# Where a hybrid decoder block copies its index queries, builds its last rotation tables and places its attention, and in which PSUM banks its feed-forward sums start

## The chip, the cores and the metric

One core of a Trainium2 chip runs the whole kernel. The metric is device time in microseconds (us) of one execution. TensorE (PE) multiplies matrices into PSUM, which the kernel divides into eight banks of 512 columns; VectorE (DVE) and ScalarE (ACT) do elementwise work; SyncE (SP) issues the DMA transfers. Each engine works through its own queue in order, so an instruction that waits holds up everything behind it on its engine.

## The reference

One decoder layer over 256 tokens of width 2048, in float32:

```
proj = h @ w_in            # u (1024), q (8x128), k (2x128), v (2x128), index q (16x64), index k (64), index w (16)
y_ssm:  S5 state-space scan over time for 64 groups of 16 channels, 64 complex states each;
        gelu, then y * sigmoid(y @ w_glu + b_glu)
y_attn: score = sum_h wi_h * relu(qi_h . ki), causal; each token keeps its 64 best keys;
        softmax over the kept keys with a distance penalty (ALiBi), 8 heads over 2 key/value heads
h = layer_norm(alpha*h + concat(y_ssm, y_attn) @ w_out)
f = (gelu(conv3(h @ w_up)) * (h @ w_gate)) @ w_down      # width 5632, causal conv of width 3
out = layer_norm(alpha*h + f)
```

## The kernel before, in words

**Number format and weights.** Every large product is made from two float32r parts of each operand, a high part (a rounded copy) and a low part (the rest), in three matmuls: high by high, low by high, high by low (`mm3`, lines 186 to 188; `wide_half`, line 206, in the feed-forward part). Weights come in 512 KB halves by DMA into one of three `raw` buffers; ACT makes the high part `wh` (line 133), DVE the low part `wl` by a subtraction (line 136). Four halves are kept ahead of their use.

**Order of the work.** Python issues the instructions in program order; a planner then lists them for each engine from its own estimates, by priority and by what is ready. `tc.high_priority()` lifts what is inside it, `tc.issue_after(x)` puts instructions behind `x` on x's engine, and `tc.manual_schedule` keeps program order on the engines that it names. Side work (the state-space job, the indexer, the GLU's inputs) is written as Python generators: `pump()` moves them on by one `yield` after each `mm3`.

**Projections.** `ws_tile` (line 310) makes one 128 x 256 column tile of the projection from 16 x 3 matmuls in one of two PSUM banks called `acc`, then issues a copy out of it (`evac`) with high priority. In order: the last two state inputs u6 and u7, eight tiles of index queries (`index_four`, line 659; here `evac` is `split`, line 180: ACT copies the high part out of the bank, DVE subtracts to get the low part, both read the bank), the index keys and weights `kw`, the keys k0, the doubled index keys `kp` (line 715, copied out to `kps` at lines 721 to 724), k1, v, and the two times four query tiles q0 and q1. `proj_tile` notes its copy in the list `evacs`.

**State-space job** (`ssm`, line 638). It goes through four blocks of channels, bi = 0 to 3. For each, `ssm_in` (line 554) moves inputs by 16 small DMAs into `ustk`, builds the rotation tables (`angles`, line 382: eight small ACT copies at line 379, two DVE operations at lines 385 and 386, three ACT operations), the decay table `dec` (eight more ACT copies at line 379), then 32 small matmuls into `bu` (line 585), then twelve DVE operations (lines 595 to 609) with two scans (602, 603), which leave the states' real and imaginary halves (line 606 ends the one, line 609 the other). `ssm_out` (line 613) multiplies them into outputs (lines 623 and 629). The tables of blocks 1 to 3 share one buffer `cs`, and all decay tables share `dec`, so a new table waits for the block before: `cs` for line 608, `dec` for line 603.

**Indexer** (line 674). For each half of the tokens it adds up 16 heads of scores (lines 694 to 702) and finds the 64 largest by eight rounds on DVE (lines 705 to 708).

**Attention and output projection.** Four pieces a00, a10, a01, a11 (head group, half of the tokens) have four steps each: `scores` (PE line 766, DVE lines 770 to 773), `weights` (ACT exponentials, DVE normalisation at line 784), `turn` (PE transposes at line 791 into a `misc` bank, ACT copies out), `values` (PE line 800). There are two `misc` banks for all of them. The output projection is a run of units, each of 6 matmuls of 512 columns (line 992); the dictionary `beside` (line 976) says ahead of which unit an attention step stands. PE's order is by hand here.

**Feed-forward part.** The first four gate blocks are computed as rows beside the end of the output projection (`gacc`, in two of the four `o` banks of pool `pso`), copied to SBUF (line 1067) and transposed into tiles `gt` of the pool `pe0`. The up and gate sums use the four banks of pool `pd`. The pools `ps` (acc and misc) and `pso` are closed before; `pe0` is opened first and so gets the four banks at the left end, `pd` the four behind, where the `o` banks were.

Of the kernel before, what the change touches and what calls it, by code (L numbers as in the profile page):

```python
# [82 lines left out]
def block_kernel(ctx: ExitStack, tc: tile.TileContext, x_t, x_n, prm_d, cst_d, ssm_d, w_u_d, w_in_d, w_kw_d, w_v_d,  # L83
# [4 lines left out]
    def pool(name, bufs=1, **kw):  # L88
        return tc.tile_pool(name=name, bufs=bufs, **kw)
# [215 lines left out]
    for _ in range(WARM):  # L305
        T.matmul(wp, lhsT=warm[:, :P], rhs=warm, start=True, stop=True)

    last_mm = []

    def ws_tile(evac, m=P):  # L310

# [6 lines left out]
            pump()  # L318
        with tc.high_priority():
            return evac(acc)  # L320

    evacs = []

    def proj_tile(name, t=None):
        if t is None:
# [10 lines left out]

    def u_tile(ct, acc):
        t = proj.tile([P, 2, P], F32, name=f"u{ct}")
        A.activation(t.rearrange("p two k -> p k two"), acc.rearrange("p (k two) -> p k two", two=2), AF.Copy)
        ut.append(t)  # L340

    bu = psb.tile([P, 2, 2, 512], F32, name="bu")
# [31 lines left out]
    def by_pair(out, a, bi, row):  # L374

        for s_ in range(2):
            for ch in range(4):
                i = bi * 8 + ch * 2 + s_
                ins = A.activation(out[:, s_, ch * 128:(ch + 1) * 128], row, AF.Copy, scale=a[:, i:i + 1])
        return ins.ins  # L380
# [173 lines left out]
    def ssm_in(bi):  # L554

        ustk = st.tile([P, 2, 2, P], F32, name="ustk")
        for c in range(2):
            for h in range(2):
                for sd in range(2):
                    q = 2 * h + sd  # L560
                    for e in range(2):
                        r = 64 * sd + 32 * e
                        nc.sync.dma_start(out=ustk[r:r + 32, c, h, :], in_=ut[2 * bi + c][32 * q:32 * q + 32, 1 - e, :])  # L563

        def t4(name):
            return st.tile([P, 2, 512], F32, name=name)

        if bi == 0:
            c, s = tab
        else:  # L570
            cs = st.tile([P, 2, 2, 512], F32, name="cs")
            c, s = cs[:, 0], cs[:, 1]
            angles(bi, c, s)
        dec = t4("dec")
        with tc.issue_after(last_angle):
            by_pair(dec, r2, bi, cc("after0"))
        yield
        bu = psb.tile([P, 2, 2, 512], F32, name="bu")
        for c_ in range(2):
            for h in range(2):  # L580
                k = (c_ * 2 + h) * 128
                for sd in range(2):
                    r = slice(64 * sd, 64 * sd + 64)
                    for ri in range(2):
                        T.matmul(bu[:, sd, ri, k:k + 128], lhsT=bt[r, 2 * bi + c_, h, ri, :], rhs=ustk[r, c_, h, :],
                                 start=True, stop=True)
                        yield
        bre, bim = bu[:, :, 0, :], bu[:, :, 1, :]
        t3, t5 = t4("t3"), t4("t5")
        if bi % 2 == 0:  # L590
            t1, t2 = t4("t1a"), t4("t2a")
        else:
            t12 = st.tile([P, 2, 2, 512], F32, name="t12b")
            t1, t2 = t12[:, 0], t12[:, 1]
        V.tensor_tensor(t1, bre, c, op=ALU.mult)
        V.tensor_tensor(t2, bim, s, op=ALU.mult)
        V.tensor_tensor(t3, bim, c, op=ALU.mult)
        V.tensor_tensor(t5, bre, s, op=ALU.mult)
        V.tensor_tensor(t1, t1, t2, op=ALU.add)
        V.tensor_tensor(t3, t3, t5, op=ALU.subtract)  # L600
        fl = lambda t: t.rearrange("p q k -> p (q k)")
        V.tensor_tensor_scan(fl(t2), fl(dec), fl(t1), initial=0.0, op0=ALU.mult, op1=ALU.add)
        V.tensor_tensor_scan(fl(t5), fl(dec), fl(t3), initial=0.0, op0=ALU.mult, op1=ALU.add)
        V.tensor_tensor(t1, t2, c, op=ALU.mult)
        V.tensor_tensor(t3, t5, s, op=ALU.mult)
        V.tensor_tensor(t1, t1, t3, op=ALU.subtract)
        V.tensor_tensor(t2, t2, s, op=ALU.mult)
        V.tensor_tensor(t5, t5, c, op=ALU.mult)
        V.tensor_tensor(t2, t2, t5, op=ALU.add)
        hs[bi] = (t1, t2)  # L610
        yield
# [47 lines left out]
    def index_four(name, low_tag):  # L659
        parts = [proj.tile([P, 4, S], F32R, name=name + n, tag=tag) for n, tag in (("h", name), ("l", low_tag))]  # L660
        tiles = [(parts[0][:, i], parts[1][:, i]) for i in range(4)]
        for h, l in tiles:
            ws_tile(lambda acc: split(h, l, acc[:, :S]))
        return tiles

    qit = index_four("qi0", "qi0l") + index_four("qi1", "q1")
# [53 lines left out]
    with tc.high_priority():  # L720
        A.activation(kps[:, :S], kp[:, :S], AF.Copy)
        for b in range(2):
            bs = slice(S + b * 128, S + b * 128 + 80)
            A.activation(kps[:, bs], kp[:, bs], AF.Copy)
    while 3 not in hs:
        next(ssm_job)
    kbd.append(st.tile([P, 2, S], F32R, name="kbdh", tag="ustk"))
# [241 lines left out]
    def row_banks(i):  # L969
# [3 lines left out]
    oacc = [row_banks(0), row_banks(1), [acc_tile() for _ in range(2)], None]  # L973
    a00.weights()
    a10.weights()
    beside = {2: a01.scores, 3: a01.weights, 6: a00.turn, 7: a10.turn, 9: a00.values, 10: a10.values,
              11: a11.scores, 12: a11.weights, 14: a01.turn, 17: a01.values, 22: a11.turn, 25: a11.values}
    unit = 0
    with tc.manual_schedule(engines={mybir.EngineType.PE}):
        for some in (range(4), range(4, 6), range(6, 8)):  # L980
# [94 lines left out]
    wx2 = ctx.enter_context(pool("wx2"))  # L1075
    ff = ctx.enter_context(pool("ff"))
    lnp = ctx.enter_context(pool("lnp"))
    pe0 = ctx.enter_context(pool("pe0", space=PSUM))
    act = ff.tile([P, NF, S], F32, name="act")
    ln_t = {}  # L1080

# [258 lines left out]
```

## Time and profile before

| what | value |
|---|---|
| median of 3 runs | 1106.2 us (1104.75 to 1106.39) |
| the profiled execution | 1107.79 us, its span 1105.8 us |
| PE busy | 1083.9 us of the span (98%), 6583 matmuls |
| DVE busy | 742.7 us (67%) |
| ACT busy | 580.4 us (52%) |
| mean granted TensorE clock | 0.994 |

The span runs from the first to the last instruction; what lies around it belongs to the execution's time. Matmuls overlap, so a busy PE need not be at its best pace. The trace names what ended each wait, by line of the kernel.

### The profile page before, as it was taken

Reading aid. Unit: us, or ns where it says so; the run is one execution under the profiler, and the core shown is the slowest. Engines: PE = TensorE matmul, PEld = TensorE weight load, DVE = VectorE, ACT = ScalarE, POOL = GpSimd, SP = SyncE. Lnnn points to the kernel's source line nnn. Section 1 sums busy time; section 2 is a strip of 40 time slices with the busy share of each in tenths; the row PEclk is TensorE's granted clock in tenths of the full one; section 3 lists DMA queues with packets and bytes.
Section 4 is the critical chain, followed back from the end, with each engine's and each line's share of the span. In section 5 each row is a group of like instructions: output and inputs, shape, how many; then the busy total and the mean of one; then the engine's idle time right before and its main releaser. Section 6 shows DMA issues by size and latency. Waiting matters only on the chain.

```text
span 1105.8 us, 16906 instructions
## 1 busy us (share of the span) xinstructions
PE 1083.9 (98%) x6583; PEld 944.7 (85%) x6583; DVE 742.7 (67%) x1067; ACT 580.4 (52%) x885; POOL 0.2 (0%) x4
## 2 busy tenths in 40 slices
PE   8999989999999999999999999999999999999997
PEld 7998879997787788888888888888888888888885
DVE  7799879887558666677565656566656546555557
ACT  5795664656544655555555555554545445445430
POOL 0000000000000000000000000000000000000000
PEclk9999989999999999999999999999999999999999
DMA  7744444446476555555765555555655566666632
GB/s 260 240 147 138 126 134 135 160 147 217 145 224 195 178 198 191 189 188 189 258 193 191 188 190 190 190 191 191 190 192 189 178 211 215 218 207 211 220 104 76
DMA packets 59887, 204.31 MB, mean 185 GB/s; under 512 B 7456, under 2 KB 10272, under 8 KB 59168
## 3 DMA queue, kind: packets, MB, share of 16 engines
q1 hardware_dynamic: 59808, 203.25, 56.2%
q8 instruction: 51, 0.84, 0.3%
q14 instruction: 28, 0.23, 0.1%
HBM read 200.07 MB, written 2.10 MB: 183 GB/s over the span
## 4 chain that ended last, share of the span: by engine, by line
PE 85%; DVE 5%; DMA 4%; SPq 2%; ACT 2%; issue 1%; ACTq 0%; DVEq 0%
PE pd L206 42%; PE e L188 7%; PE e L186 7%; PE e L187 7%; PE acc L187 4%; PE acc L186 4%; PE acc L188 4%; PE o L186 2%; PE o L187 2%; PE o L188 2%; SPq L563 2%; DMA raw<-in_w_out_dram 2%; DVE wl L136 1%; DMA raw<-in_w_u_dram 1%; PE ibanks L694 1%
## 5 line engine op out<-in xcount | busy, mean ns | idle before, releaser
L136 DVE TENSOR_TENSOR wl<-raw,wh 128x1024 fp32r<-128x1024 f32 (+1 forms) x297 | 362.2, 1220 | 251.9 <-ACT wh L133 249.5
L133 ACT ACTIVATE wh<-raw 128x1024 fp32r<-128x1024 f32 (+1 forms) x297 | 313.7, 1057 | 268.0 <-PE pd L206 132.5
L206 PE MATMUL pd<-mix,wh 128*128 128x512 f32 x1344 | 321.4, 391 | 0.7 <-ACT gate L1067 0.7
L206 PEld LDWEIGHTS pd<-mix,wh 128*128 128x128 f32 x1344 | 246.8, 188 | 48.8 <-ACT gate L1067 1.1
L206 PEld LDWEIGHTS pd<-mix,wl 128*128 128x128 f32 x1344 | 172.4, 191 | 6.6
L206 PE MATMUL pd<-mix,wl 128*128 128x256 f32 x1344 | 174.8, 283 | 0.0
L186 PE MATMUL acc<-x,wh 128*128 128x256 f32 (+1 forms) x368 | 105.9, 289 | 6.5 <-ACT kv L327 3.7
L187 PE MATMUL acc<-x,wl 128*128 128x256 f32 (+1 forms) x368 | 105.6, 287 | 0.6 <-DVE wl L136 0.5
L188 PE MATMUL acc<-x,wh 128*128 128x256 f32 (+1 forms) x368 | 105.3, 286 | 0.0
L136 DVE TENSOR_TENSOR wxl<-raw,wxh 128x1024 fp32r<-128x1024 f32 x42 | 51.4, 1225 | 42.9 <-ACT wxh L133 40.1
L186 PEld LDWEIGHTS acc<-x,wh 128*128 128x128 f32 (+1 forms) x368 | 70.5, 192 | 8.0 <-ACT kv L327 3.8
L133 ACT ACTIVATE wxh<-raw 128x1024 fp32r<-128x1024 f32 x42 | 44.5, 1061 | 54.6 <-DMA raw<-in_w_down_dram 36.4
L187 PEld LDWEIGHTS acc<-x,wl 128*128 128x128 f32 (+1 forms) x368 | 70.7, 192 | 2.1 <-DVE wl L136 0.7
L188 PEld LDWEIGHTS acc<-x,wh 128*128 128x128 f32 (+1 forms) x368 | 70.6, 192 | 1.0 <-issue 0.8
L187 PE MATMUL e<-wh,acthl 128*128 128x512 f32 (+1 forms) x154 | 59.5, 386 | 0.0
L186 PE MATMUL e<-wh,acthl 128*128 128x512 f32 (+1 forms) x154 | 59.4, 387 | 0.0
L188 PE MATMUL e<-wl,acthl 128*128 128x512 f32 (+1 forms) x154 | 58.7, 386 | 0.0
L175 ACT ACTIVATE hc<-hc 128x256 f32<-128x256 f32 x44 | 18.4, 418 | 75.5 <-DVE hc L1108 75.5
L186 PE MATMUL e<-wxh,acthl 128*128 128x512 f32 (+1 forms) x130 | 50.1, 386 | 0.0
L187 PE MATMUL e<-wxh,acthl 128*128 128x512 f32 (+1 forms) x130 | 50.1, 386 | 0.0
L188 PE MATMUL e<-wxl,acthl 128*128 128x512 f32 (+1 forms) x130 | 50.1, 386 | 0.0
L211 DVE TENSOR_TENSOR sum<-sum,pd 128x256 f32<-128x256 f32 x84 | 34.8, 414 | 0.0
(315 smaller groups left out, 1507.6 us busy)
## 6 DMA issues: line engine op xcount, KB each, us to landing
raw<-in_w_gate_dram SPq DMA_DIRECT2D x88, 512.0 KB, 4.4
raw<-in_w_up_dram SPq DMA_DIRECT2D x88, 512.0 KB, 4.5
raw<-in_w_down_dram SPq DMA_DIRECT2D x88, 512.0 KB, 4.9
raw<-in_w_in_dram SPq DMA_DIRECT2D x40, 512.0 KB, 4.3
raw<-in_w_out_dram SPq DMA_DIRECT2D x32, 512.0 KB, 4.0
raw<-in_w_u_dram SPq DMA_DIRECT2D x9, 512.0 KB, 5.6
raw<-in_w_glu_dram SPq DMA_DIRECT2D x8, 512.0 KB, 3.6
raw<-in_w_v_dram SPq DMA_DIRECT2D x4, 512.0 KB, 4.3
```

The costliest lines, as they stand in the source:

```text
L133: A.activation(h[:, :w], raw[:, :w], AF.Copy)
L136: last_wl[:] = [V.tensor_sub(l[:, :w], raw[:, :w], h[:, :w].bitcast(F32)).ins]
L175: ins = A.activation(*args, **kw)
L186: T.matmul(out, lhsT=lh[0], rhs=rh[0], start=start, stop=False)
L187: T.matmul(out, lhsT=lh[1], rhs=rh[0], start=False, stop=False)
L188: return T.matmul(out, lhsT=lh[0], rhs=rh[1], start=False, stop=stop).ins
L206: ins = T.matmul(out[:, 0] if low else out, lhsT=w, rhs=r, start=kh == 0 and i == 0, stop=kh == 1 and i == 15)
L211: V.tensor_tensor(t, t, hi, op=ALU.add)
L563: nc.sync.dma_start(out=ustk[r:r + 32, c, h, :], in_=ut[2 * bi + c][32 * q:32 * q + 32, 1 - e, :])
L694: T.matmul(out, lhsT=q, rhs=k, start=i == 0, stop=i == 2)
```

## The change

Five edits:

1. `index_four`: ACT copies the whole tile out of its bank into a buffer `whole` (two buffers of the tag `rel` in SBUF) with high priority; `split` then reads this buffer, outside the high priority. These copies and those of the state inputs are noted in `evacs`, too.
2. `ssm_in`: the tables of blocks 1 and 2 stay where they were but go behind the last noted copy; block 3 pauses after its `bu` matmuls until the index keys' copies are issued, and its tables are issued then. The decay table of every block is issued after the `bu` matmuls, behind the last noted copy.
3. The `kps` copies are noted, and the flag `keys` is set.
4. `beside`: a01's scores and weights go from units 2 and 3 to 9 and 10; the transposes of a00 and a10 from 6 and 7 to 7 and 8; the other steps go one to three units later.
5. Pool `pe0` is taken from the right end of PSUM, so that `pd` gets the left four banks.

```diff
--- before.py
+++ after.py
@@ -305,7 +305,7 @@
     for _ in range(WARM):
         T.matmul(wp, lhsT=warm[:, :P], rhs=warm, start=True, stop=True)
 
-    last_mm = []
+    last_mm, evacs = [], []
 
     def ws_tile(evac, m=P):
 
@@ -319,8 +319,6 @@
         with tc.high_priority():
             return evac(acc)
 
-    evacs = []
-
     def proj_tile(name, t=None):
         if t is None:
             t = proj.tile([P, S], F32, name=name)
@@ -336,7 +334,7 @@
 
     def u_tile(ct, acc):
         t = proj.tile([P, 2, P], F32, name=f"u{ct}")
-        A.activation(t.rearrange("p two k -> p k two"), acc.rearrange("p (k two) -> p k two", two=2), AF.Copy)
+        evacs.append(A.activation(t.rearrange("p two k -> p k two"), acc.rearrange("p (k two) -> p k two", two=2), AF.Copy).ins)
         ut.append(t)
 
     bu = psb.tile([P, 2, 2, 512], F32, name="bu")
@@ -565,15 +563,16 @@
         def t4(name):
             return st.tile([P, 2, 512], F32, name=name)
 
-        if bi == 0:
-            c, s = tab
-        else:
+        def turns():
+            if bi == 0:
+                return tab
             cs = st.tile([P, 2, 2, 512], F32, name="cs")
-            c, s = cs[:, 0], cs[:, 1]
-            angles(bi, c, s)
-        dec = t4("dec")
-        with tc.issue_after(last_angle):
-            by_pair(dec, r2, bi, cc("after0"))
+            with tc.issue_after(evacs[-1]):
+                angles(bi, cs[:, 0], cs[:, 1])
+            return cs[:, 0], cs[:, 1]
+
+        if bi < 3:
+            c, s = turns()
         yield
         bu = psb.tile([P, 2, 2, 512], F32, name="bu")
         for c_ in range(2):
@@ -585,6 +584,14 @@
                         T.matmul(bu[:, sd, ri, k:k + 128], lhsT=bt[r, 2 * bi + c_, h, ri, :], rhs=ustk[r, c_, h, :],
                                  start=True, stop=True)
                         yield
+        if bi == 3:
+
+            while "keys" not in state:
+                yield
+            c, s = turns()
+        dec = t4("dec")
+        with tc.issue_after(evacs[-1] if bi else last_angle):
+            by_pair(dec, r2, bi, cc("after0"))
         bre, bim = bu[:, :, 0, :], bu[:, :, 1, :]
         t3, t5 = t4("t3"), t4("t5")
         if bi % 2 == 0:
@@ -660,7 +667,10 @@
         parts = [proj.tile([P, 4, S], F32R, name=name + n, tag=tag) for n, tag in (("h", name), ("l", low_tag))]
         tiles = [(parts[0][:, i], parts[1][:, i]) for i in range(4)]
         for h, l in tiles:
-            ws_tile(lambda acc: split(h, l, acc[:, :S]))
+
+            whole = at.tile([P, 512], F32, name="qi", tag="rel", bufs=2)[:, :S]
+            evacs.append(ws_tile(lambda acc: A.activation(whole, acc[:, :S], AF.Copy)).ins)
+            split(h, l, whole)
         return tiles
 
     qit = index_four("qi0", "qi0l") + index_four("qi1", "q1")
@@ -721,7 +731,8 @@
         A.activation(kps[:, :S], kp[:, :S], AF.Copy)
         for b in range(2):
             bs = slice(S + b * 128, S + b * 128 + 80)
-            A.activation(kps[:, bs], kp[:, bs], AF.Copy)
+            evacs.append(A.activation(kps[:, bs], kp[:, bs], AF.Copy).ins)
+    state["keys"] = True
     while 3 not in hs:
         next(ssm_job)
     kbd.append(st.tile([P, 2, S], F32R, name="kbdh", tag="ustk"))
@@ -973,8 +984,8 @@
     oacc = [row_banks(0), row_banks(1), [acc_tile() for _ in range(2)], None]
     a00.weights()
     a10.weights()
-    beside = {2: a01.scores, 3: a01.weights, 6: a00.turn, 7: a10.turn, 9: a00.values, 10: a10.values,
-              11: a11.scores, 12: a11.weights, 14: a01.turn, 17: a01.values, 22: a11.turn, 25: a11.values}
+    beside = {7: a00.turn, 8: a10.turn, 9: a01.scores, 10: a01.weights, 11: a00.values, 12: a10.values,
+              13: a11.scores, 14: a11.weights, 17: a01.turn, 20: a01.values, 24: a11.turn, 27: a11.values}
     unit = 0
     with tc.manual_schedule(engines={mybir.EngineType.PE}):
         for some in (range(4), range(4, 6), range(6, 8)):
@@ -1075,7 +1086,7 @@
     wx2 = ctx.enter_context(pool("wx2"))
     ff = ctx.enter_context(pool("ff"))
     lnp = ctx.enter_context(pool("lnp"))
-    pe0 = ctx.enter_context(pool("pe0", space=PSUM))
+    pe0 = ctx.enter_context(pool("pe0", space=PSUM, side="right"))
     act = ff.tile([P, NF, S], F32, name="act")
     ln_t = {}
```

## Rows read from the trace of the kernel before

**Rows 1.** The page, busy time: engine, us (share of span), instructions.
```profile
PE 1083.9 (98%) x6583; PEld 944.7 (85%) x6583; DVE 742.7 (67%) x1067; ACT 580.4 (52%) x885; POOL 0.2 (0%) x4
```
**Rows 2.** Waits of PE: engine, line, releaser: us in total, times, longest.
```profile
PE acc L186 <- ACT kv L327: 3.7, 1, 3.7
PE misc L791 <- DVE e L770: 2.7, 1, 2.7
PE acc L186 <- DVE qi1l L182: 2.2, 2, 1.6
...
PE pd L206 <- ACT gate L1067: 0.7, 1, 0.7
```
**Rows 3.** Chain of waits, feed-forward stretch: start, us, what.
```profile
413.05 441.75 PE pd L206 x2537
```
**Rows 4.** Windows: stretch, length, busy us (instructions) by engine, PE clock, DMA, GB/s.
```profile
146.60:151.20 4.60, 4.60 (x21) 4.60 (x22) 4.60 (x5) 2.40 (x8) 0.00 (x0) 0.50 0.37 118
151.20:153.60 2.40, 2.40 (x22) 2.40 (x21) 2.04 (x4) 1.82 (x4) 0.00 (x0) 1.00 0.38 67
266.40:270.40 4.00, 4.00 (x16) 3.30 (x17) 3.05 (x5) 1.79 (x3) 0.00 (x0) 0.61 0.55 170
```
**Rows 5.** Timeline of PE, projections: start, us, line, operation, count [idle before, releaser].
```profile
116.23 0.42 PE L629 MATMUL misc<-t12b,cbd 128*32 128x128 f32 x8
...
146.59 0.58 PE L186 MATMUL acc<-x,wh 128*128 128x256 f32 x1 [3.69 <-ACT kv L327]
...
154.07 0.42 PE L629 MATMUL misc<-t1a,cbd 128*32 128x128 f32 x8
...
191.15 0.43 PE L629 MATMUL misc<-t12b,cbd 128*32 128x128 f32 x8
```
**Rows 6.** Timeline of DVE, projections.
```profile
111.02 0.41 DVE L182 TENSOR_TENSOR qi1l<-acc,qi1h 128x256 fp32r<-128x256 f32 x1
...
114.75 1.21 DVE L606 TENSOR_TENSOR t12b<-t12b,t 128x1024 f32<-128x1024 f32 x1
...
119.62 1.21 DVE L609 TENSOR_TENSOR t12b<-t12b,t 128x1024 f32<-128x1024 f32 x1
...
148.24 1.22 DVE L606 TENSOR_TENSOR t1a<-t1a,t 128x1024 f32<-128x1024 f32 x1
149.37 1.22 DVE L608 TENSOR_TENSOR t<-t,cs 128x1024 f32<-128x1024 f32 x1
...
165.21 1.23 DVE L595 TENSOR_TENSOR t12b<-bu,cs 128x1024 f32<-128x1024 f32 x1 [3.25 <-ACT cs L175]
...
177.62 0.33 DVE L701 SCALAR_TENSOR_TENSOR score<-rel,wi,cst 128x128 f32<-128x128 f32 x1
...
187.39 1.22 DVE L606 TENSOR_TENSOR t12b<-t12b,t 128x1024 f32<-128x1024 f32 x1
```
**Rows 7.** Timeline of ACT around the key tiles.
```profile
143.83 2.45 ACT L379 ACTIVATE dec<-cst,r 128x128 f32<-128x128 f32 x8 [3.40 <-DVE t L603]
146.18 0.36 ACT L327 ACTIVATE kv<-acc 128x256 f32<-128x256 f32 x1
```
**Rows 8.** Line 182's operations: duration ns min/median/max, first and last start, shape.
```profile
L182 DVE TENSOR_TENSOR yl<-y,yh x8: 419/420/425, 201.3 to 206.6; 128x256 fp32r<-128x256 f32 x8
...
L182 DVE TENSOR_TENSOR qi1l<-acc,qi1h x4: 412/412/414, 111.0 to 133.3; 128x256 fp32r<-128x256 f32 x4
```
**Rows 9.** Timeline of PE at the start of the output projection.
```profile
256.27 1.89 PE L766 MATMUL misc<-kv,q 128*128 128x256 f32 x8
257.80 0.58 PE L186 MATMUL o<-wh,mix 128*128 128x512 f32 x1
```
**Rows 10.** Timeline of DVE, the same stretch.
```profile
260.37 0.86 DVE L784 TENSOR_SCALAR e<-e,rs 128x128 f32<-128x128 f32 x4
...
263.60 0.87 DVE L784 TENSOR_SCALAR e<-e,rs 128x128 f32<-128x128 f32 x4
...
265.52 0.75 DVE L770 SCALAR_TENSOR_TENSOR e<-misc,score 128x256 f32<-128x256 f32 x2
```

## The prediction

> **What bounds the kernel now.** I read the page's busy times first: PE works for 1083.9 of the 1105.8 us of the span [rows 1], so little can come off, and only where PE stands still or runs at half clock. The waits of PE come next [rows 2]. Four of them are touched by the change: 3.7 us for the copy of k0 out of its bank, 2.7 us at the transposes of a00, 2.2 us in two waits for the low part of an index query, and 0.7 us at the first feed-forward sum. The reader is to see that three of the four end on DVE in truth: the copy of k0 stood on ACT behind the eight `dec` pieces, and these had waited 3.40 us for a scan of line 603 [rows 7]. The windows show the rest of the price: after the 3.7 us wait the granted clock is 0.50 from 146.6 to 151.2, and 0.61 on the mean from 266.4 to 270.4 after the 2.7 us wait [rows 4]: the lower of the two levels, 1.2 instead of 2.4 GHz. Last the chain of waits: from 413 on it is 441.75 us of feed-forward matmuls without a break [rows 3]. What PE gains before that, it keeps.
>
> **The change part by part.**
>
> *Index queries.* Before, a bank comes free only when DVE has subtracted from it, and DVE's queue was full of block 1's work: the subtraction that PE waited for ran at 111.02 [rows 6]. With the copy on ACT the bank is free after one copy of about 0.36 us (as for k0 [rows 7]). Removed: 2.2 us [rows 2]. Added: eight ACT copies, 8 x 0.36 = 2.9 us of ACT, which is busy 52% of the span [rows 1]; I cost them at nothing, because another bank is being filled for 5.2 us meanwhile (a tile's 48 matmuls at 2.40/22 = 0.11 us, the pace of the window at full clock [rows 4]). If that cover were gone, 2.9 us would come on top. The subtraction itself does not get shorter: 412 ns from the bank, 420 ns for the same shape from SBUF [rows 8]. The Trainium skill says in "VectorE: DVE Perf Modes", Rules for kernel authors, that one should copy PSUM to SBUF first if one will do many operations on a matmul's output, and else accept the slower read. Here two operations follow, so by that rule the copy costs 2.9 us and returns nothing; the 2.2 us of waiting say otherwise.
>
> What is late next: the state-space outputs. Block 1's first matmul of line 629 starts at 116.23 [rows 5], and its input is done at 114.75 + 1.21 = 115.96 [rows 6]: 0.27 us of slack. The first query wait (1.6 us of the 2.2) lies before it. If DVE's work does not move, 1.3 us come back as a wait there. Ends: 0 if the planner puts these matmuls later, 1.3 if not; I take 1.3, since DVE has the same work to do before. Left of this edit: 0.9 us.
>
> *Tables behind the keys.* Moved on ACT past the copies of k0 and of the keys, for block 3: sixteen small pieces (2.45 us for eight [rows 7]), three table operations, and on DVE the two of lines 385 and 386; no DMA is among them (`ustk` stays where it was), so SP's queue is not touched, and POOL has none. The copy of k0 then has nothing before it that waits for a scan: 3.7 us go [rows 2]. With them goes the half clock: 21 matmuls in 4.60 us, where the next window does 22 in 2.40 [rows 4], so 2.3 us. Together 6.0 us, and PE would be 6.9 ahead with the 0.9 from above.
>
> What is late next: block 2's outputs start at 154.07 [rows 5], their input ends at 148.24 + 1.22 = 149.46 [rows 6]: slack 4.61 us. Again the ends are 0 (matmuls put later) and 6.9 - 4.6 = 2.3 us (DVE unmoved); I take 2.3. PE is then 4.6 ahead. Block 3: output at 191.15, input at 187.39 + 1.22 = 188.61, slack 2.54; but DVE had stood 3.25 us at line 595 for the cosines of block 3 [rows 6], and ACT, which makes them, need no longer wait for a late PE to give weight buffers free. 2.54 + 3.25 is more than 4.6, so I add nothing. Were none of that wait recovered, 2.1 us would be lost.
>
> *Attention's places.* PE stood at a00's transposes until DVE had done line 770 at 265.52 + 0.75 [rows 10], which is not a00's own input but a01's scores, in the same two `misc` banks. With the scores behind both transposes the banks are free. What ends last then is the normalisation: for a00 260.37 + 0.86 = 261.23, for a10 264.47 [rows 10]. PE's side on the same clock: a01's scores leave (1.53 us from 256.27 to 257.80 [rows 9]); unit 5 ended 2.7 us before the release at 266.3, at 263.6, so one of the four units since 257.80 takes 1.45 us. Five units from 256.27 end at 263.5: a00 has 2.3 us in hand. a10 comes a unit later, at 265.0 or after: 0.5 us in hand. I take no wait; the ends are 0 and the old 2.7. Saved are 2.7 us and the half clock's part: 0.39/0.5 of 4.0 us is 3.1 us at half level, half of it lost, 1.6 [rows 4]. Together 4.3. The later steps keep room: a01 has eight units (11.6 us) from scores to transposes, and its values stand four units ahead of the matmul that needs them. The scores' own PE time only moves.
>
> *Banks.* The first feed-forward sum lay in the bank that ACT was still copying `gacc` from: 0.7 us [rows 2]. On the left it gets the former `acc` banks, last read long before. The transposed gate tiles go to the right, and wait for that copy anyway. 0.7 us.
>
> *Sum.* 0.9 + 6.0 - 2.3 + 4.3 + 0.7 = 9.6 us. The profiled execution took 1107.79 us (2.0 around its span), so it would take 1098.2; the median of the runs is 1.6 lower, and from it the forecast is 1106.2 - 9.6 = 1096.6 us.
>
> **The rivals.**
>
> *All of it comes off.* The planner puts the output matmuls behind what their inputs need, and no later wait forms: 2.2 + 6.0 + 4.3 + 0.7 = 13.2, 1093.0 us. For it: the order on PE is listed anew. Against: DVE was late already, in three of four waits.
>
> *The last table blocks ACT.* `cs` of block 3 waits for line 608 of block 2, done at 149.37 + 1.22 = 150.59 [rows 6]. If ACT's queue has it ahead of the copy of k1, that copy ends at 150.59 + 2.45 + 0.36 = 153.4. PE, 0.9 ahead of the 142.9 at which its wait began (146.59 - 3.69 [rows 5]), would end k1 at 142.0 + 5.2 and 12 matmuls of v (1.3) at 148.5, and then need the bank: 4.9 us in place of the 2.3 that I took, and 2.3 for the clock. 9.6 + 2.3 - 4.9 - 2.3 = 4.7 off: 1101.5 us. For it: the same happened with `dec` [rows 7]. Against: a copy has high priority.
>
> *The copy's buffer takes the bank's place.* Outside the high priority the subtractions can fall behind all of block 1's work, to 119.62 + 1.21 = 120.83 [rows 6]; with two buffers the third copy then ends at 120.83 + 0.41 + 0.36 = 121.6. PE's next tile starts where the first wait began (111.02 + 0.41 - 1.6 = 109.8) and would end at 115.0, so PE stands 6.6 us instead of 2.2, with a clock loss like the 2.3 above: 6.7 lost, 0.7 more than the keys bring. Attention and banks leave 5.0 - 0.7 = 4.3 off: 1101.9 us. Against: later work of normal priority, such as line 701, does get between two scans [rows 6].
>
> *Copies that ACT has no room for.* The whole 2.9 us fall on PE: 6.7 off, 1099.5 us.
>
> *Slower: block 3 comes too late.* Its twelve DVE operations can no longer be issued ahead of the keys. PE can't pass 191.15 before their input is there [rows 5]. If it comes d later than in the profile, PE is d - 2.54 behind the kernel before at that point, whatever it gained earlier, with 2.3 for a clock drop; 5.0 follow from attention and banks. The kernel is slower from d = 5.2 on, and by over 0.2% from 7.4. With d = 10: 2.7 + 2.1 = 4.8 slower, 1111 us. For it: the job's pause, and a low place for it on DVE, where weights and the indexer's sums press. Against: its tables ran after the keys in the profile, too.
>
> *It doesn't do what it says.* The planner orders otherwise, and new waits of the same size form: 1106 us.
>
> **How the numbers follow.** Forecast 0.36; all off 0.22; last table 0.12; buffer 0.09; ACT's room 0.03; nothing 0.07; slower 0.11. A measurement of this kernel can tell about 0.2% (2.2 us) from no change. Faster: 0.36 + 0.22 + 0.12 + 0.09 + 0.03 = 0.82; same 0.07; slower 0.11. The range goes from 1091 (all off, and 2 more) to 1106: outside are the slower case, half of "nothing" and some 0.03 below, about 0.18.
>
> **What would show it.** Right: no PE wait for `qi` at line 182, for `kv` at line 327, for line 770 and for line 1067; granted clock 1.00 from 100 to 400; waits of line 629 for `t12b` or `t1a` of 1 to 2 us each, near 115 and 149; the feed-forward stretch as long as before, some 10 us earlier. Wrong: PE idle for `q` copies or `rel` (buffer), ACT idle at `cs` for line 608 with `kv` behind it (last table), a long wait of line 629 in block 3 (slower), a feed-forward stretch with breaks.

## The result, and the profile after

The changed kernel takes 1096.5 us (median of 4 runs, 1094.98 to 1098.76), the kernel before 1105.89 us beside it: ratio 0.9918 [0.9897, 0.9939]. A second measurement on one chip with three variants (a1 below) gave 0.9915 [0.9902, 0.9929]. The forecast was 1096.6. The sum was right; three of its five terms were not: the two losses expected at the state-space outputs hardly came, and the gain at attention's places was well below its forecast. Most of what follows is about these.

The page of the changed kernel, busy time. PE's busy time fell by 3.6 us, mostly matmuls that no longer run at half clock; its share rose because the span fell by 10.3 us. It answers to [rows 1].

```profile
PE 1080.3 (99%) x6583; PEld 941.3 (86%) x6583; DVE 743.0 (68%) x1067; ACT 582.9 (53%) x893; POOL 0.2 (0%) x4
```

The waits of PE in the changed kernel, against [rows 2]: the copy of k0, the transposes of a00, the low part of the queries and the first feed-forward sum are all gone. New are 1.3 us at line 777 (line 766 before: the scores of a later step) and, smaller, 0.6 us for line 757 (the copy of v). The 1.5 us for line 136 lie in the first 50 us, ahead of all that the edits touch.

```profile
PE acc L187 <- DVE wl L136: 1.7, 2, 1.5
PE e L1230 <- DVE diag L1226: 1.7, 1, 1.7
PE misc L306 <- DVE warm L303: 1.4, 1, 1.4
PE o L186 <- DVE z L907: 1.4, 1, 1.4
PE misc L777 <- DVE mix L182: 1.3, 1, 1.3
PE bu L187 <- DVE wl L136: 0.7, 1, 0.7
PE acc L186 <- ACT kv L757: 0.6, 1, 0.6
```

The chain of waits in the feed-forward stretch: as long as in [rows 3] to the hundredth, 10.40 us earlier.

```profile
402.65 441.75 PE pd L206 x2537
```

Windows of the changed kernel, over the two stretches that ran below full clock in [rows 4] (the work in them has moved; the third figure from the right is PE's granted clock, 1.00, the higher level of 2.4 GHz):

```profile
146.60:151.20 4.60, 4.60 (x44) 4.25 (x44) 4.60 (x6) 2.60 (x8) 0.00 (x0) 1.00 0.39 114
264.00:270.00 6.00, 5.95 (x23) 3.92 (x21) 4.51 (x10) 4.10 (x12) 0.00 (x0) 1.00 0.54 182
```

**Where PE gains and where it gives back.** The table subtracts, for the same matmul, its start in each kernel's PE timeline from its start in the kernel before; one column for each landmark, headed by its start before. The first landmark lies in the query tiles before the first old wait: what stands there is start-up, not the change.

```
             query tile  key copies  first of v  gated unit  last of      first feed-
                                                 ends        projection   forward sum
start before     103.54      141.92      155.01      255.22      384.84       385.92
changed            0.37        2.94        9.19        7.80        9.41        10.27
a1 (the same)      0.57        3.12        9.38        8.37        9.35        10.21
e1 queries         0.21        2.56        1.39        1.38        2.44         2.45
e2 tables          2.57        3.10        9.58        8.66        7.03         7.04
e3 places          1.03        1.27        0.19        0.18        2.68         2.68
e4 banks           0.59        1.51        1.43        1.43        2.34         3.19
g1                 0.11        0.75        7.22        6.31        8.07         8.08
g2                -0.35        2.43        1.38        0.45        3.72         4.58
h1                 0.95        3.70        2.39        1.42        4.31         5.16
h2                 1.81        4.21       10.46        7.86        9.80        10.65
f3                 2.14        3.96       10.21        8.48       10.22        11.08
f1                 1.16        3.81       10.07        8.79       12.32        13.17
f4                 0.74        3.42        9.68        8.26       12.91        13.77
```

Read along the second line: queries 2.94 - 0.37 = 2.6 us, keys 9.19 - 2.94 = 6.3 less the 1.4 given back up to the gated unit's end, attention and projection 1.6, banks 0.86; 10.27 - 0.37 = 9.9 in all. The second execution (a1) gives 2.6, 6.3 less 1.0, 1.0 and 0.86. How far one such difference can be trusted the line of e4 shows: up to the feed-forward part it is the kernel before, yet it has 1.51 - 0.59 = 0.9 us of lead at the key copies (the last section comes back to this).

### The profile page after: what moved, and what is told of

The parts are those of the page before. It is cut to its first block, busy times and chain, and to the rows that moved or that the text cites. A ratio compares the mean times of both kernels' runs of the same rounds, so it can differ in the third digit from the quotient of the medians.

```text
span 1095.5 us, 16909 instructions
## 1 busy us (share of the span) xinstructions
PE 1080.3 (99%) x6583; PEld 941.3 (86%) x6583; DVE 743.0 (68%) x1067; ACT 582.9 (53%) x893; POOL 0.2 (0%) x4
## 4 chain that ended last, share of the span: by engine, by line
PE 71%; DMA 2%; DVE 2%; ACT 0%; issue 0%; ACTq 0%; DVEq 0%
PE pd L206 43%; PE e L186 7%; PE e L187 7%; PE e L188 7%; DMA raw<-in_w_out_dram 2%; PE o L186 2%; PE o L187 2%; PE o L188 2%; PE misc L942 0%; DVE wl L136 0%; PE acc L188 0%; PE acc L186 0%; PE acc L187 0%; ACT wh L133 0%; DVE z L1217 0%; DVE wxl L136 0%
## 5 line engine op out<-in xcount | busy, mean ns | idle before, releaser
L186 PE MATMUL acc<-x,wh 128*128 128x256 f32 (+1 forms) x368 | 104.3, 286 | 0.6 <-ACT kv L757 0.6
L188 PE MATMUL acc<-x,wh 128*128 128x256 f32 (+1 forms) x368 | 104.0, 283 | 0.0
L186 PEld LDWEIGHTS acc<-x,wh 128*128 128x128 f32 (+1 forms) x368 | 69.4, 189 | 1.6 <-ACT kv L757 0.8
L186 PE MATMUL e<-wh,acthl 128*128 128x512 f32 (+1 forms) x154 | 59.4, 387 | 0.0
L186 PE MATMUL e<-wxh,acthl 128*128 128x512 f32 (+1 forms) x130 | 50.1, 386 | 0.0
```

Source lines behind the costliest of these rows:

```text
L186: T.matmul(out, lhsT=lh[0], rhs=rh[0], start=start, stop=False)
L188: return T.matmul(out, lhsT=lh[0], rhs=rh[1], start=False, stop=stop).ins
```

## The experiments

**Each edit alone.** e1 has the query copies only, e2 the tables only (with the pause of block 3 and the issuing behind the last copy), e3 attention's places only, e4 the banks only. All four were timed on one chip beside a kernel before of 1106.45 us.

```diff
 # e1
-            ws_tile(lambda acc: split(h, l, acc[:, :S]))
+            whole = at.tile([P, 512], F32, name="qi", tag="rel", bufs=2)[:, :S]
+            evacs.append(ws_tile(lambda acc: A.activation(whole, acc[:, :S], AF.Copy)).ins)
+            split(h, l, whole)
 # e2
+            with tc.issue_after(evacs[-1]):
+                angles(bi, cs[:, 0], cs[:, 1])
...
+            while "keys" not in state:
+                yield
...
+        with tc.issue_after(evacs[-1] if bi else last_angle):
 # e3
-    beside = {2: a01.scores, 3: a01.weights, 6: a00.turn, 7: a10.turn, ...
+    beside = {7: a00.turn, 8: a10.turn, 9: a01.scores, 10: a01.weights, ...
 # e4
-    pe0 = ctx.enter_context(pool("pe0", space=PSUM))
+    pe0 = ctx.enter_context(pool("pe0", space=PSUM, side="right"))
```

> Edit 1 alone. Theory A (the freed bank): the two waits of 2.2 us at line 182 go, and PE is 2 to 3 us ahead where the index keys begin; the copy of k0 still stands behind the decay table, so part or all of that is lost there: 1103.5 to 1106. Theory B (what came off ahead of the keys in the changed kernel came from block 1's tables being made 3.4 us earlier on ACT, not from the bank): without edit 2 block 1's first DVE operation stays near 96, the output matmul of line 629 waits 1 us or more near 115, and nothing comes off: 1105.5 to 1107. Rival (the copy's buffer holds ACT up): ACT idle before the copy of a query, slower than 1107.

e1 measured 1104.42 us, 0.9977 [0.9967, 0.9986]. PE is 2.4 us ahead at the key copies (2.56 - 0.21) and loses half of it at k0, whose copy still stands on ACT behind the `dec` pieces. First the waits of PE in e1, then ACT's timeline around the copy:

```profile
PE acc L186 <- ACT kv L327: 4.4, 1, 4.4
PE misc L793 <- DVE e L772: 2.7, 1, 2.7
```
```profile
141.93 2.45 ACT L379 ACTIVATE dec<-cst,r 128x128 f32<-128x128 f32 x8 [4.28 <-DVE t L603]
144.28 0.36 ACT L327 ACTIVATE kv<-acc 128x256 f32<-128x256 f32 x1
```

The scan (line 603) sets when the copy runs, and it didn't move as far as PE did; so the wait grew from 3.7 to 4.4 us. That is the pattern of e1, and of e2 below: part of what the edit gains the next old wait takes.

> Edits 2 and 3 alone. Theory A: the wait for the copy of k0 (3.7) and the half clock after it (2.3) go, the query waits of about 2 us stay: 1100 to 1102. Theory B: block 1's tables come early here too, and 8 us or more are gained by the keys: 1097 to 1098.5. By my prediction, where 2.3 come back at block 2's outputs: 1102.2.

e2 measured 1105.1 us, 0.9983 [0.9972, 0.9993]. The wait for k0 is gone, PE is 8.66 us ahead at the gated unit's end (2.57 of it start-up), and then stands at a00's transposes longer than ever. The wait in e2, and the operation of DVE that ends it:

```profile
PE misc L800 <- DVE e L779: 5.9, 1, 5.9
```
```profile
259.55 0.42 DVE L716 TENSOR_TENSOR score<-score,cst 128x256 f32<-128x256 f32 x1
260.00 1.42 DVE L779 SCALAR_TENSOR_TENSOR e<-misc,score 128x256 f32<-128x256 f32 x4
```

Line 779 needs the score table that the search for the largest values (ending with line 716) leaves on DVE. It came 5.5 us earlier than before (260.00 against 265.52 [rows 10]), PE over 8: the difference is the longer wait. The profiled execution is e2's fastest (1100.92); the other 11 took 1102.4 to 1105.93, and what they lose beyond this trace stays open.

> Edit 4 alone. My prediction: no wait at the transposes, clock 1.00, 4.3 us off: 1101.6. By the trace of the changed kernel: a wait of about 1.3 us at a11's scores for the subtraction that empties a10's bank, which stands on DVE behind a01's normalisation, and some 0.5 at the unit ahead of the transposes: 2.1 us off, 1103.8.

e3 measured 1104.41 us, 0.9979 [0.9967, 0.9991]. The wait of a00's transposes is gone, the one for k0 stays (4.1 us), and the new one at the scores is there with this edit alone, so it belongs to the places and to nothing else. Waits of PE in e3:

```profile
PE acc L186 <- ACT kv L327: 4.1, 1, 4.1
...
PE misc L766 <- DVE mix L182: 1.4, 1, 1.4
```

> Edit 5 alone. Both: the wait of 0.7 us at the first feed-forward sum goes and nothing else moves: 1105.2 on the median, within what can be measured; the trace shows the feed-forward sums starting 0.7 to 0.9 us after the last row matmul earlier than before. Rival: another bank's last reader takes its place, and the wait stays.

e4 measured 1105.84 us, 0.9991 [0.9978, 1.0004]: the time alone doesn't tell it from no change. In the trace the wait for the gate's copy is gone, and PE gains 3.19 - 2.34 = 0.85 us at just that matmul.

**Pairs and triples.** g1 is e2 and e3 together. g2 is e1, e3 and e4, with the diffs shown for these: the changed kernel without the tables.

```diff
 # g1: the changed kernel with
-            whole = at.tile([P, 512], F32, name="qi", tag="rel", bufs=2)[:, :S]
-            evacs.append(ws_tile(lambda acc: A.activation(whole, acc[:, :S], AF.Copy)).ins)
-            split(h, l, whole)
+            ws_tile(lambda acc: split(h, l, acc[:, :S]))
...
-    pe0 = ctx.enter_context(pool("pe0", space=PSUM, side="right"))
+    pe0 = ctx.enter_context(pool("pe0", space=PSUM))
```

> The tables (edits 2 and 3) and attention's places (edit 4) alone; queries and banks as before. Theory A (the edits are tied: what the tables gain was lost at a00's transposes, whose bank DVE frees at a fixed time, and the places take that away): the lead of 8.7 us at the end of the gated unit's matmuls is kept through attention, some 10 us in all less the bank's 0.9, 1097 to 1098.5 us. Rival B (the edits are independent, the parts add up): 1.9 + 2.3 us as measured alone, 1102 us.

g1 measured 1097.71 us, 0.9915 [0.9903, 0.9928]. Alone the two bring 1.4 and 2.0 us, together 10.3 (1108.01 - 1097.71, the kernel before on this chip): the edits are tied, as theory A has it. The tables move PE forward, the places take away the wait that stood against it. In the trace of g1 the two waits that its missing edits would remove are still there:

```profile
PE acc L186 <- DVE qi1l L182: 1.5, 2, 0.9
...
PE pd L206 <- ACT gate L1075: 0.7, 1, 0.7
```

By the table the changed kernel is some 2 us ahead of g1 (9.9 against 8.0 at the first sum, start-up taken off). The times don't show it: 0.9915 for both, on two chips, each uncertain by 0.13%. What the queries and the banks add to these two edits is thus read from the traces alone.

> Queries, attention's places and banks (edits 1, 4 and 5); the tables of blocks 1 to 3 as before. Theory A (without the tables the query's gain ends at k0's copy, which stands on ACT behind pieces that wait for a scan on DVE): the wait for k0's copy is 4 to 4.5 us with the half clock after it, PE's lead is 1.4 us from there to the gated unit, and places and banks bring 2.1 and 0.9 us on top: 4.4 off, 1101.5 to 1102.5 us. Rival B (the query copies carry most of the changed kernel's 10 us once the later waits are gone): 1098 us or less. Then the tables would matter little.

g2 measured 1103.11 us, 0.9961 [0.9948, 0.9975]: without the tables more than half of the change is missing. Its wait for k0:

```profile
PE acc L186 <- ACT kv L327: 4.2, 1, 4.2
```

**The pause of block 3.** h1 is the changed kernel without it; the tables are still issued behind the last copy.

```diff
-        if bi < 3:
-            c, s = turns()
+        c, s = turns()
...
-        if bi == 3:
-            while "keys" not in state:
-                yield
-            c, s = turns()
```

> The changed kernel without the pause of block 3 for the keys: its tables are issued like those of blocks 1 and 2, still behind the last copy out of a bank. Theory A (the pause is needed: with block 3 in the stream, the decay pieces of block 2 stand on ACT ahead of k0's copy again, waiting for the scan of block 1): a wait of PE for k0's copy of 3 to 4.5 us, half clock behind it, 5 to 6 us slower than the changed kernel, 1101 to 1103 us. Rival B (issuing behind the last copy does it, the pause only moves block 3's own tables): no such wait, within 1 us of the changed kernel; then block 3's cosines may hold k1's copy for up to 2 us.

h1 measured 1102.21 us, 0.9956 [0.9942, 0.9969], beside 1097.47 for the changed kernel on this chip (a1): the pause is worth 4.7 us; issuing behind the last copy is not enough. Without the pause the `dec` of block 3 stands ahead of k0's copy again, and waits for the scan of block 2 (the expectation names one block too early for both). ACT in h1, and PE's clock in the window behind the wait:

```profile
140.90 2.45 ACT L377 ACTIVATE dec<-cst,r 128x128 f32<-128x128 f32 x8 [4.32 <-DVE t L604]
143.25 0.37 ACT L325 ACTIVATE kv<-acc 128x256 f32<-128x256 f32 x1
```
```profile
144.00:148.00 4.00, 4.00 (x20) 4.00 (x20) 4.00 (x5) 2.08 (x8) 0.00 (x0) 0.50 0.39 135
```

**The price of the query copies.** h2 makes each of the eight twice.

```diff
-            evacs.append(ws_tile(lambda acc: A.activation(whole, acc[:, :S], AF.Copy)).ins)
+            evacs.append(ws_tile(lambda acc: [A.activation(whole, acc[:, :S], AF.Copy) for _ in range(2)][-1]).ins)
```

> The changed kernel with each copy of an index query out of its bank made twice by ACT (eight more copies of 0.36 to 0.39 us, 3 us of ACT). Theory A (ACT's copies are hidden, since PE fills another bank for 5.2 us meanwhile): no wait of PE for a query's bank, within 0.7 us of the changed kernel. Rival B (ACT has no room in this stretch): up to 3 us slower, as waits of PE for the copy or for weights that ACT converts later.

h2 measured 1097.56 us, 0.9928 [0.9914, 0.9943]; a1 took 1097.47 beside it. No wait for a query's bank appears: 3 us more of ACT here cost nothing that can be measured. (Its 0.6 us at the indexer's scores, which a1 hasn't, stands in g2 and h1 too, 0.7 us each.) The cover that the prediction named holds.

**The changed kernel again**, for the comparisons on that chip.

> The changed kernel as it is, beside the next three on one chip: 0.992 of the time before, with the 1.3 us wait at a11's scores and no wait for k0's copy, for a query's low part, for a00's transposes or for the first feed-forward sum.

a1 measured 1097.47 us, 0.9915 [0.9902, 0.9929].

**Why the outputs' waits did not come.** The prediction let PE wait 1.3 us in block 1 and 2.3 us in block 2 for the state-space outputs. In the changed kernel DVE starts block 1 at 92.72 instead of 96.11, since ACT makes the cosines of block 1 ahead of a weight conversion; in the kernel before they were behind it, and it waited 1.86 us for its DMA. ACT, then DVE, in the kernel before:

```profile
92.74 1.06 ACT L133 ACTIVATE wh<-raw 128x1024 fp32r<-128x1024 f32 x1 [1.86 <-DMA raw<-in_w_in_dram]
...
94.94 1.13 ACT L175 ACTIVATE cs<-cs,cst 128x1024 f32<-128x1024 f32 x1
```
```profile
96.11 1.23 DVE L595 TENSOR_TENSOR t12b<-bu,cs 128x1024 f32<-128x1024 f32 x1 [1.05 <-ACT cs L175]
```

ACT and DVE in the changed kernel; lines 602 and 613 are 595 and 606 of before [rows 6]:

```profile
91.55 1.14 ACT L175 ACTIVATE cs<-cs,cst 128x1024 f32<-128x1024 f32 x1
92.59 0.66 ACT L641 ACTIVATE y<-misc 128x256 f32<-128x256 f32 x2
93.14 1.04 ACT L133 ACTIVATE wh<-raw 128x1024 fp32r<-128x1024 f32 x1
```
```profile
92.72 1.22 DVE L602 TENSOR_TENSOR t12b<-bu,cs 128x1024 f32<-128x1024 f32 x1 [0.61 <-ACT cs L175]
...
112.50 1.23 DVE L613 TENSOR_TENSOR t12b<-t12b,t 128x1024 f32<-128x1024 f32 x1
...
147.53 1.22 DVE L613 TENSOR_TENSOR t1a<-t1a,t 128x1024 f32<-128x1024 f32 x1
...
183.28 1.23 DVE L613 TENSOR_TENSOR t12b<-t12b,t 128x1024 f32<-128x1024 f32 x1
```

And the output matmuls on PE (line 636, 629 before [rows 5]), none with a wait:

```profile
114.17 0.43 PE L636 MATMUL misc<-t12b,cbd 128*32 128x128 f32 x8
...
148.81 0.43 PE L636 MATMUL misc<-t1a,cbd 128*32 128x128 f32 x8
...
186.67 0.43 PE L636 MATMUL misc<-t12b,cbd 128*32 128x128 f32 x8
```

Block 1's input is done at 113.73, 0.44 us ahead of PE; block 2's at 148.75, 0.06 ahead; block 3's at 184.51, 2.2 ahead.

The two blocks that were charged differ in why. Block 1's input comes 2.2 us sooner than before (115.96 to 113.73), and its outputs stand at almost the same place in PE's order, behind 520 `acc` matmuls instead of 518: here the earlier chain did it. Block 2's input comes only 0.7 us sooner (149.46 to 148.75). What moved are its outputs: in the kernel before they stand ahead of the first matmul of v (154.07 [rows 5] against 155.01), in the changed kernel 3 us behind it (148.81 against 145.82). The first matmul of v, before and changed:

```profile
155.01 0.28 PE L186 MATMUL acc<-wh,x 128*128 128x256 f32 x1
```
```profile
145.82 0.28 PE L186 MATMUL acc<-wh,x 128*128 128x256 f32 x1
```

At their old place, behind 720 `acc` matmuls, PE would have come to them at about 145.4 and waited 3.3 us, by an estimate from these rows (the 720th starts at 145.22); they now stand behind 748. So for block 2 the planner's order kept the wait away. It goes with the pause of block 3: every kernel that has the pause has these outputs behind 744 to 750 `acc` matmuls, every other one, h1 among them, behind 720. And e2 and g1, which make block 1's cosines about as late as the kernel before, have no wait there either (input some 0.15 us ahead in both).

Which edit moved block 1? With the start-up of each execution added back, block 1's first operation starts at 92.4 to 93.3 in every kernel with the query copies in their place (changed, a1, e1, g2, h1, h2, f1, f4) and at 95.0 to 96.1 in every one without (before, e2, e3, e4, g1). So the query edit moved the cosines, and the reading that it takes the tables to do it falls. f3 puts the old order of ACT back into the changed kernel, by recording these cosines eight steps later.

```diff
+        if bi == 1:
+            for _ in range(8):
+                yield
+            with tc.issue_after(state["wh"]):
+                cosines(c)
         dec = t4("dec")
```

> The changed kernel with the cosines of block 1 recorded eight steps later, so that ACT takes one more weight conversion, the one that waits for its DMA, ahead of them, as in the kernel before. Theory A (the predicted waits of the outputs stayed out only because ACT made these cosines some 3.4 us earlier): block 1's first operation on DVE starts near 95.5 to 96 instead of 92.72, the input of block 1's outputs is done near 116 instead of 113.73, and PE waits there for t12b for 0.5 to 2 us; the lead at the key copies falls from 2.9 to between 1 and 2.4 us, and the kernel is 0.5 to 2 us slower than the changed one: 1097 to 1098.5 us. Rival B (the outputs' matmuls simply stand later in PE's list than their inputs): no wait for t12b, 1096.5 us.

f3 measured 1096.23 us, 0.9895 [0.9881, 0.9908]: no slower than the changed kernel, so the price was missed. The mechanism shows in the trace. f3's start-up was 1.8 us ahead of the changed kernel's execution (2.14 against 0.37); block 1 starts at 92.83, or 95.0 with the start-up added back, among the kernels without the copies, and PE now waits at the outputs. DVE and PE of f3:

```profile
92.83 1.22 DVE L611 TENSOR_TENSOR t12b<-bu,cs 128x1024 f32<-128x1024 f32 x1 [1.06 <-ACT cs L175]
...
111.48 1.22 DVE L622 TENSOR_TENSOR t12b<-t12b,t 128x1024 f32<-128x1024 f32 x1
```
```profile
112.76 0.43 PE L645 MATMUL misc<-t12b,cbd 128*32 128x128 f32 x8 [0.64 <-DVE t12b L622]
```

There is one more wait of 0.2 us, for `t1a`. Not all of the two is the cosines' doing: in f3 the planner also put the outputs of block 1 three and those of block 2 four `acc` matmuls sooner than in the changed kernel, some 0.4 and 0.5 us at 0.12 us each. With start-up taken off f3 is 0.8 us behind at the key copies (1.8 against 2.6) and 1.0 behind at the first feed-forward sum (8.9 against 9.9). So the predicted wait can form, and where it was put, but at 0.64 and 0.2 it is a quarter of the 3.6 us that were charged, and nothing that the medians show.

**The scores of a11.** In the changed kernel they take the bank from which DVE has yet to empty a10's values (line 811; the turned weights, which the expectation of f1 names, ACT copies out). DVE's order there, then PE:

```profile
268.30 1.14 DVE L795 TENSOR_SCALAR e<-e,rs 128x256 f32<-128x256 f32 x4
269.35 1.22 DVE L136 TENSOR_TENSOR wl<-raw,wh 128x1024 fp32r<-128x1024 f32 x1
270.49 0.69 DVE L182 TENSOR_TENSOR mix<-misc,mix 128x512 fp32r<-128x512 f32 x1
```
```profile
271.23 1.13 PE L777 MATMUL misc<-kv,q 128*128 128x256 f32 x4 [1.28 <-DVE mix L182]
```

The emptying (line 182) is queued behind the normalisation of a01 (line 795) and a weight's low part. f1 puts the scores and weights one unit later, f4 two.

```diff
-              13: a11.scores, 14: a11.weights, 17: a01.turn, ...
+              14: a11.scores, 15: a11.weights, 17: a01.turn, ...   # f1
+              15: a11.scores, 16: a11.weights, 17: a01.turn, ...   # f4
```

> The changed kernel with a11's scores and weights one unit later (units 14 and 15 instead of 13 and 14). In the changed kernel's trace the scores of a11 stood 1.28 us for a bank that DVE empties of a10's turned weights only at 270.49, behind the normalisation of a01 (1.14 us) and a weight's low part (1.22 us). Theory A (that queue on DVE is the whole cost): a unit of 1.45 us is more than the 1.28, the wait at the scores goes, PE is 1.3 us further ahead at the end of attention, 1095.2 us. Rival B (the scores come when DVE is full whatever the unit, the wait goes along with them or a value matmul becomes late): no gain, 1096.5 us, a wait of 1 us or more still at the scores or at a11's values.

f1 measured 1094.31 us, 0.9884 [0.9870, 0.9897]. The wait shrinks to 0.3 us, no other near it takes its place, and at the first feed-forward sum PE is 2.1 us further ahead than in the changed kernel (12.0 against 9.9, start-up taken off). The changed kernel was not timed on this chip; f3, which has the scores at their old place, took 1096.23 here, 1.9 us more than f1:

```profile
PE misc L777 <- DVE mix L182: 0.3, 1, 0.3
```

> The changed kernel with a11's scores and weights two units later (units 15 and 16). One unit later their wait was 0.33 us, the same bank emptied at 269.90 + 0.68. Theory A (that bank's emptying behind the normalisation of a01 on DVE is all there is): no wait at the scores, PE 1.3 us further ahead than the changed kernel at the end of attention, 0.1 to 0.25% faster than the changed kernel on the same chip. Rival B (the gain of the earlier placement test was the start-up, not the scores): the same time as the changed kernel within 0.1%, or a wait for a11's turned weights in its place.

f4 measured 1094.24 us, 0.9892 [0.9878, 0.9905], beside 1097.47 of a1: 3.2 us or 0.3% faster, and the fastest of all versions by its profiled span (1091.9 us). The emptying and the scores on DVE and PE of f4, without a wait:

```profile
270.12 0.68 DVE L182 TENSOR_TENSOR mix<-misc,mix 128x512 fp32r<-128x512 f32 x1
```
```profile
271.17 1.89 PE L777 MATMUL misc<-kv,q 128*128 128x256 f32 x8
```

That is more than theory A's 1.3 us. In f1 and f4 the wait `PE o L186 <- DVE z` is missing too, which is 1.4 us in the changed kernel and 1.7 in a1, some 55 us later. One weight conversion also stands earlier on ACT and DVE in both; that it is what frees that bank in time was not tried by itself. Nor is it shown that the two runs miss this wait for the scores' sake: it is 1.1 us in the kernel before, 0.1 in e4 with the same order of instructions up to there, and 0.5 in h2, so it changes from one execution to the next. The interval of f4's ratio still touches that of a1, so "faster than the changed kernel" rests on both, f1 and f4, and on their traces.

## Why the prediction was right, point by point

*Index queries: 0.9 predicted, 2.6 found.* The removal and the cover (h2) were right, but the 2.2 us is the high end: the same two waits take 1.0, 1.7, 1.2 and 1.5 us in e2, e3, e4 and g1, which read the bank as the kernel before does. The step "I take 1.3, since DVE has the same work to do before" failed: the DVE had the same work, but began it 3 us sooner, because the same edit reordered ACT. The end that was set aside, 0, was the right one, though not for its reason (the planner putting the matmuls later: it put them 2 later). The row that could have said so stood in the trace of before: ACT idle for 1.86 us on a DMA ahead of the cosines.

On the copies themselves, the Trainium skill's "VectorE: DVE Perf Modes", Rules for kernel authors, would accept the slower read where few operations follow. The runs show what that leaves out here: it isn't DVE's reading time (412 against 420 ns [rows 8]) but the time for which the bank is held; e1 and h2 show waits that go and copies that cost nothing.

*Keys: 6.0 gross predicted, 6.3 found; 3.7 net predicted, 4.9 (a1: 5.3) found.* Wait and half clock went as worked out [rows 2, 4]. Block 2's wait of 2.3 us did not come. The step that failed is the choice of that end ("DVE unmoved"): DVE hardly moved, by 0.7 us, but the planner put the outputs 28 matmuls later, which is the reason that the prediction gives for its other end, 0. What was given back instead, 1.0 to 1.4 us, is in small pieces up to the gated unit's end, of which 0.6 (a1: 0.2) is the copy of v. Some 0.4 of it, and of the 6.3, is block 2's eight output matmuls themselves, which crossed the landmark at v. The rival that the last table blocks ACT was half right: `cs` of block 3 did hold ACT for 2.00 us, but behind the copy of k1, so nobody waited:

```profile
146.62 0.35 ACT L325 ACTIVATE kv<-acc 128x256 f32<-128x256 f32 x1
...
149.92 2.46 ACT L377 ACTIVATE cs<-cst,f 128x128 f32<-128x128 f32 x8 [2.00 <-DVE t L615]
```

*Attention's places: 4.3 predicted, 1.6 (a1: 1.0) found.* a00 and a10 have no wait, as worked out. The step that failed is "the later steps keep room": it looked at when inputs are ready (a01's eight units, the values' four) and not at when the `misc` banks come free. The very argument that explained the old wait, a bank held by another step, applied again one step on: 1.28 us at a11's scores. Besides, PE is now early enough to wait 0.5 us in unit 6, in two short waits for an input of the projection itself (`mix`, lines 181 and 182), and the wait for `z` is 0.3 (a1: 0.6) us longer than before. 4.3 - 1.28 - 0.5 - 0.3 = 2.2 (a1: 1.9), so 0.6 to 0.9 us more is not assigned.

*Banks: 0.7 predicted, 0.86 found*, and 0.85 in e4.

*The sum*: 9.6 predicted. The profiled executions differ by 1107.79 - 1097.41 = 10.4, the medians by 9.4. The terms are off by +1.7, +1.2 (+1.6), -2.7 (-3.3) and +0.2: they cancel, and that forecast and median lie 0.1 us apart is luck. That the two executions differ by 1 us more than the medians has to do with the trace that the terms were read from: next to e4's it is a slow one (last section).

*All of it comes off* was met at the outputs, for block 2 by the very order that it names, and failed at attention's places. *The slower rival* (block 3 too late): its inputs came 2.2 us ahead of PE, so its condition was not met. *Nothing*, *ACT's room* and *the copy's buffer* are excluded by the waits and by h2.

## What to carry to other kernels

Waits in a chain are not independent: single edits worth 1.4 and 2.0 us were worth 10 together, since what the first gains is mostly lost at the next wait, whose releaser hasn't moved as far, unless the second takes that wait away. When an edit brings one engine forward, check the next waits for their releasers, and whether the edit itself reorders the queue in which these stand, on the engine that releases as on the one that waits. When a step is moved between others that share banks, follow each bank to its next user, not only each input to its consumer.

## What was not expected of the hardware

The granted clock fell after some waits of PE and not after others, and the length of the wait alone doesn't say which. It was 0.50, the level of 1.2 GHz, behind waits of 3.7 us [rows 4] and of 4.5 us (h1), 0.61 on the mean of a stretch behind 2.7 us [rows 4], and 1.00 behind the 1.37 us that PE waits for `z` in the changed kernel:

```profile
327.00:331.00 4.00, 3.46 (x15) 2.90 (x16) 4.00 (x6) 1.06 (x1) 0.00 (x0) 1.00 0.60 198
```

In e1 PE waits 2.7 us at the same transposes, and behind this wait, which ends at 264.93, the clock stays at 1.00:

```profile
264.50:268.50 4.00, 3.57 (x20) 3.03 (x21) 3.42 (x7) 2.15 (x3) 0.00 (x0) 1.00 0.59 175
```

So the 1.6 us that the prediction took for the half clock there is lost in some traces (before, e4) and not in others.

Up to the query tiles, code that e3 and e4 share with the kernel before ran 1.03 and 0.59 us sooner than in it, and over all profiled executions the same matmul starts 0.35 us later to 2.57 us sooner. That is as much as single terms of the sum: terms have to be read between two landmarks, never from a profile's end. Nor is that exact. ACT, DVE and PE run the same instructions in the same order in e4 and in the kernel before up to the feed-forward sums, yet e4 gains 0.9 us up to the key copies (its query waits are 1.2 instead of 2.2 us) and 0.9 us more from the gated unit's end to the last of the projection (its wait for `z` is 0.1 instead of 1.1 us). Counted from e4's trace, the changed kernel's 2.6 us at the queries would be some 1.6, its 1.6 at attention some 0.7, and its 9.9 in all 8.1, with the medians' 9.4 in between. Terms of under 1 us need more than one trace on either side.
